# The first feed-forward product in block products of 256 columns, and sums of weight quadrants by adding DMAs

## The chip, the core and the metric

The kernel runs on one core of a Trainium2 chip. A core has five engines that run side by side, each with its own queue of instructions: TensorE (matmuls, PE in the profile, its weight loads PEld), VectorE (DVE), ScalarE (ACT), GpSimd (POOL) and SyncE (SP, which here only issues DMAs). The metric is the device time of one execution in microseconds; lower is better.

## The reference

One layer of a hybrid decoder: 512 tokens (S) of 1,024 channels (D), all in 32-bit floats.

```python
def hybrid_layer(x, norm1_w, w_in, ..., w_out, norm2_w, w_ff1, w_ff2, rel_bias):
    h = rmsnorm(x, norm1_w)
    proj = h @ w_in
    ...
    mix = jnp.concatenate([y_a.reshape(Bsz, S, A_WIDTH), y_b, y_c.reshape(Bsz, S, C_WIDTH)], axis=-1)
    x = x + mix @ w_out
    h2 = rmsnorm(x, norm2_w)
    x = x + jnp.square(jax.nn.relu(h2 @ w_ff1)) @ w_ff2
    return x
```

`y_a`, `y_b`, `y_c` are dilated attention, gated linear attention and block-sparse attention. A last RMSNorm follows. `w_ff1` is 1,024 x 4,096 and `w_ff2` 4,096 x 1,024. The change concerns the last line, from `h2` on.

## The kernel before

**Precision.** Every large product is made of three matmuls. A factor is split into a high part (rounded to a shorter format, by ScalarE) and a low part (what is left, by VectorE), and high x high, high x low and low x high are summed in PSUM. Splitting a weight tile of 128x1024 ("a cut", `parts`, lines 302 to 318) is one `wh` by ScalarE and one `wl` by VectorE. At most five cut pairs are alive (`WPAIRS`).

**The planner.** The order of every engine's queue is settled when the kernel is built. `Plan` (lines 105 to 202) runs some dozens of generators ("streams") that yield operations, waits for named events, and takes of counted resources (PSUM banks, cut pairs, large tiles). At each step it issues the operation that could start first by its cost formulas (lines 46 to 87), by priority among equals. So an edit of one stream can move instructions of others. All instructions are issued from one line (L137 in the profile), and rows are told apart by tile names. `order` rows below are this written order.

**Buffers.** 27 tiles of 128x1024 (`BIGS`, name tag "big") and 34 of 128x512 (`SLOTS`) are handed round.

**The stages.** Attention and its projections come first, until 191.9 us. Then `ff2(0)`, lines 1356 to 1401, multiplies the mixed heads by `w_out`. `y_out` (lines 1075 to 1094) transposes the normed tokens to `yh`, `yl`. `ffn` (lines 1313 to 1354) follows: the first product in 32 blocks `f` of 128 output columns, each of 8 k-tiles x 3 matmuls with all 512 tokens as the moving side (`f<-yh,wh 128x512`). Only blocks 0 to 3 go in two halves of 256 tokens, so as to start on the tokens that are ready first: 192 matmuls of 256 columns. The other 28 blocks are 672 matmuls of 512. `h_out` puts relu and square of a block into `h` tiles.

**The second product.** `w_ff2` is taken in four pieces c = 1 to 4 of 1,024 rows; `w_out` is c = 0. `ff2(c)` is a Strassen-Winograd product: two by two blocks, seven block products (24 matmuls of 512 columns each) where eight would be plain. The left factors are sums of the quadrants of `h` (`a_parts`, lines 1103 to 1178: `s` tiles, cut into `Ah`, `Al`), the right factors are sums of quadrants of the weights. Those sums, eight of 128x1024 per piece, are VectorE operations in `sums2` (lines 399 to 427): `w2raw<-w2raw`, `t<-w2raw`, `w2raw<-t,w2raw`, `w2raw<-w2raw,t`. The seven products accumulate in PSUM banks called `f2X`, `f2Y`, `f2Z`, `f2W`; VectorE adds a bank to the result rows `x` where Winograd's sums ask for it (`add`, lines 1183 to 1199), while later products go on in the same bank. `ff2(c)` for c = 1 to 3 comes after block f = 8c, `ff2(4)` after block 31.

**Loads.** SyncE's queue loads weights in 512 KB tiles: `wraw` for the first product (`fetch`, line 285), eight `w2raw` per piece (`fetch2`, lines 341 to 351). GpSimd's queue issues only a few small loads early on.

Of the kernel before, what the change touches and what calls it, by code (L numbers as in the profile page):

```python
# [28 lines left out]
BIGS, SLOTS, WPAIRS, SCRATCH = 27, 34, 5, 4096  # L29
NC = 5  # L30
# [3 lines left out]
def part_name(ap):  # L34
    name = ap.tensor.name
    if name[:2] in ("xh", "xl"):
        return f"{name}:{ap.offset // 512 % 4}"
    if name[:2] in ("yh", "yl"):
        return f"{name}:{ap.offset // 256 % 2}"
    return name  # L40


class Op:


    def __init__(self, eng, method, args, kw):
# [159 lines left out]
def hybrid_block_kernel(ctx: ExitStack, tc: tile.TileContext, x0_d, xT_d, x_d, w0_d, wv_d, wqk_d, w1_d, w2_d,  # L206
# [9 lines left out]
    plan = Plan(nc, dict(BANKS, raw=3, w=WPAIRS, big=BIGS, raw2=8, part=5, lev=4, cnt=1, few=1))  # L216
# [31 lines left out]
    cst = consts.tile([128, 1028], F32)  # L248
    ident = cst[:, 0:128]
    hsel = cst[:, 128:132]  # L250
    bmask = cst[:, 132:388]
    smask = cst[:, 388:900]
    flip = cst[:, 900:1028]
    lmask = consts.tile([128, len(LEVELS), 64], I32)
# [5 lines left out]
    gw = consts.tile([128, 256], F32)  # L260
# [9 lines left out]
    plan.free["big"].pop()  # L270
# [3 lines left out]
    xh, xl = ([t[:, k] for t in (quarters(n, F32R), quarters(n, F32R)) for k in range(4)] for n in ("xh", "xl"))  # L274
# [49 lines left out]
    def cut():  # L324
        for key, src, n in pieces:
            if key[0] in ("x", "x3"):
                continue
            yield ("wait", ("raw", key))
            yield from parts(key, raws.pop(key), n)
            give("raw")  # L330
            give("big")
            if key[0] == "1" and (key[1] % 8 == 0 and key[1] or key[1] == 31):
                yield from cut2((key[1] + 7) // 8)
            if key == ("v", 1, 3):
                yield from cut2(0)

# [4 lines left out]
    def fetch2():  # L341
        yield ("wait", ("raw", ("1", 5)))
        for c in range(1, NC):
            for q in ((0, 0), (1, 0), (1, 1), (0, 1)):
                for ip in range(2):
                    yield ("take", "raw2")
                    yield ("take", "big")
                    t = quads[c, q, ip] = big("w2raw")
                    yield SP.dma_start(t, w2_d[c, q[0], q[1], ip])
                fire(("quad", c, q))  # L350
            spawn(sums2(c), 4)
# [47 lines left out]
    def sums2(c):  # L399

        for q in ((0, 0), (1, 0), (1, 1), (0, 1)):
            yield ("wait", ("quad", c, q))
        b11, b12, b21, b22 = ([quads.pop((c, q, ip)) for ip in range(2)] for q in ((0, 0), (0, 1), (1, 0), (1, 1)))
        t2 = [None, None]
        B[c] = {0: b11, 1: b21, 5: b22, 3: b12, 2: t2, 4: b11, 6: b21}
        for n in (0, 1, 5):
            fire(("B", c, n))
        if c == NC - 1:
            yield ("prio", 2)
# [5 lines left out]
        fire(("B", c, 2))  # L415
        fire(("B", c, 3))
        yield ("wait", ("cut2", c, 0))
        for ip in range(2):
            yield DVE.tensor_tensor(b11[ip], t2[ip], b11[ip], op=OP.subtract)
        fire(("B", c, 4))  # L420
        yield ("wait", ("cut2", c, 1))
        for ip in range(2):
            yield DVE.tensor_tensor(b21[ip], b21[ip], t2[ip], op=OP.subtract)
        fire(("B", c, 6))
        yield ("wait", ("cut2", c, 2))
        give("big")
        give("big")

    B = {}

    def products(c):


        if not c:
            return ((0, "X", True, ((0, 0),)), (4, "W", True, ((1, 1),)), (6, "W", False, ((1, 0),)), (2, "X", False, ((1, 0),)),
                    (3, "X", False, ((1, 1),)), (1, "Y", True, ((0, 0),)), (5, "X", False, ((0, 1),)))
        if c < NC - 1:
            return ((0, "X", True, ((0, 0),)), (1, "Y", True, ((0, 0),)), (2, "X", False, ((0, 1),)), (3, "Z", True, ((1, 1),)),
                    (4, "X", False, ((1, 1),)), (5, "Z", False, ((0, 1),)), (6, "X", False, ((1, 0),)))
        return ((0, "X", True, ((0, 0),)), (4, "W", True, ((1, 1),)), (1, "Y", True, ((0, 0),)), (6, "W", False, ((1, 0),)),  # L440
                (2, "X", False, ((1, 0),)), (3, "X", False, ((1, 1),)), (5, "X", False, ((0, 1),)))

    def cut2(c):
        for o, (n, *_) in enumerate(products(c)):
# [58 lines left out]
    def load_small():  # L503
        yield ("wait", "zeros")
        for t, d in ((cst, cst_d), (rbx[:32], rb_d[:32]), (rb[64:67, :12], rb_d[32:]), (bav, ba_d), (wax[:16], wa2_d)):
# [65 lines left out]
    vB = [slot(f"vB{i}", shape=(128, 2, 256)) for i in range(2)]  # L571
    vS = {}
# [996 lines left out]
```

## Time and profile before

| what | value |
|---|---|
| median of 3 runs | 579.65 us (579.02, 579.65, 580.02) |
| the profiled execution's own time | 580.01 us |
| its span, first to last instruction | 577.9 us |
| mean granted TensorE clock | 0.999 |
| first product, blocks 4 to 31 | 672 matmuls of 512 columns |
| second product, each piece | 168 matmuls of 512 columns |

The span leaves out 2.1 us around it. The busy share of an engine is a mean over stages; what a stage is worth is read from the chain of waits (the work that ended last, followed back) and from windows of the stage. In a row of a group, "busy us, mean ns | idle before <- releaser" follows the shape; the mean of one operation includes a part that overlaps with the next one, so the distance between starts of operations that stand back to back is a little shorter. Granted clock and DMA share run from 0 to 1.

### The profile page before, as it was taken

To read this page: it belongs to the slowest core of one execution; us is meant where nothing else is said; L and a number is where in the kernel's file an instruction comes from. 1 tells how busy PE (TensorE), PEld (TensorE's weight loads), DVE (VectorE), ACT (ScalarE), POOL (GpSimd) and SP (SyncE) were. 2 spreads that over 40 slices of the span, in tenths; PEclk is the share of its full clock that TensorE was granted. 3 is DMA by queue.
4 is the path that set the end of the run, shared out by engine and by line. 5 is a ranking of instruction groups with operands and counts; after the bars stand their busy time and mean duration, and the time that the engine had idled before them with its cause. 6 is when DMAs were issued, how large, how long until landed. Compare 5 with 4: busy or idle time off the path is not lost.

```text
span 577.9 us, 8055 instructions
## 1 busy us (share of the span) xinstructions
PE 569.4 (99%) x3006; PEld 474.8 (82%) x3006; DVE 444.5 (77%) x774; ACT 329.3 (57%) x575; POOL 18.7 (3%) x36
## 2 busy tenths in 40 slices
PE   9999999999999999999999999999999999999995
PEld 8987888878888678899888888888888888888884
DVE  6879999897887889965399854599834698772995
ACT  6755566887777476636285435375253664273654
POOL 7100000000000000000000000000000000000021
PEclk9999999999999999999999999999999999999999
DMA  8921213430621435822007721028520057001004
GB/s 306 389 77 38 74 44 122 128 96 15 251 79 37 131 124 155 319 75 73 1 7 240 224 76 36 2 76 265 158 85 0 1 182 219 36 1 36 1 0 146
DMA packets 20838, 62.51 MB, mean 108 GB/s; under 512 B 2498, under 2 KB 3184, under 8 KB 20800
## 3 DMA queue, kind: packets, MB, share of 16 engines
q1 hardware_dynamic: 19872, 60.37, 31.9%
q0 software_dynamic: 640, 1.10, 0.6%
q8 instruction: 24, 0.39, 0.3%
q10 hardware_dynamic: 288, 0.53, 0.2%
q14 instruction: 14, 0.11, 0.1%
HBM read 59.86 MB, written 2.13 MB: 107 GB/s over the span
## 4 chain that ended last, share of the span: by engine, by line
PE 96%; DMA 2%; DVE 1%; issue 0%; ACT 0%; DVEq 0%
PE f L137 30%; PE f2X L137 17%; PE qkps L137 11%; PE vps L137 8%; PE f2Z L137 6%; PE f2Y L137 4%; PE f2W L137 4%; PE sps L137 3%; PE ptp L137 2%; PE po L137 2%; PE av L137 2%; DMA w2raw<-in_w 2%; PE lp L137 1%; PE bk L137 1%; PE bq L137 1%; PE op L137 1%
## 5 line engine op out<-in xcount | busy, mean ns | idle before, releaser
L137 PE MATMUL f<-yh,wh 128*128 128x512 f32 (+1 forms) x288 | 105.7, 367 | 0.0
L137 PE MATMUL f<-yl,wh 128*128 128x512 f32 (+1 forms) x288 | 105.5, 366 | 0.2 <-DVE yl L137 0.2
L137 PE MATMUL f<-yh,wl 128*128 128x512 f32 (+1 forms) x288 | 105.4, 366 | 0.0
L137 DVE TENSOR_TENSOR wl<-w2raw,wh 128x1024 fp32r<-128x1024 f32 x48 | 59.4, 1244 | 52.4 <-ACT wh L137 30.3
L137 DVE TENSOR_TENSOR wl<-wraw,wh 128x1024 fp32r<-128x1024 f32 (+1 forms) x60 | 68.4, 1152 | 24.5 <-ACT wh L137 24.3
L137 ACT ACTIVATE wh<-wraw 128x1024 fp32r<-128x1024 f32 (+1 forms) x59 | 58.0, 1002 | 30.4 <-PE f2X L137 18.6
L137 ACT ACTIVATE wh<-w2raw 128x1024 fp32r<-128x1024 f32 x48 | 50.4, 1054 | 32.9 <-PE f L137 14.5
L137 PE MATMUL f2X<-wh,Ah 128*128 128x512 f32 (+1 forms) x160 | 62.3, 390 | 0.0
L137 PE MATMUL f2X<-wl,Ah 128*128 128x512 f32 (+1 forms) x160 | 61.9, 387 | 0.0
L137 PE MATMUL f2X<-wh,Al 128*128 128x512 f32 (+1 forms) x160 | 61.9, 387 | 0.0
L137 PEld LDWEIGHTS f<-yl,wh 128*128 128x128 f32 x288 | 54.4, 189 | 9.1 <-DVE yl L137 0.4
L137 PEld LDWEIGHTS f<-yh,wl 128*128 128x128 f32 x288 | 54.3, 189 | 8.8
L137 PEld LDWEIGHTS f<-yh,wh 128*128 128x128 f32 x288 | 54.4, 189 | 8.7
L137 ACT ACTIVATE h<-f 128x512 f32<-128x512 f32 x32 | 19.0, 594 | 68.9 <-PE f L137 68.8
L137 PE MATMUL qkps<-xh,wh 128*128 128x512 f32 x96 | 39.2, 408 | 0.0
L137 PE MATMUL qkps<-xh,wl 128*128 128x512 f32 x96 | 37.6, 392 | 0.0
L137 PE MATMUL qkps<-xl,wh 128*128 128x512 f32 x96 | 37.5, 391 | 0.0
L137 PEld LDWEIGHTS f2X<-wh,Ah 128*128 128x128 f32 x160 | 30.1, 188 | 7.6 <-issue 1.6
L137 PEld LDWEIGHTS f2X<-wl,Ah 128*128 128x128 f32 x160 | 30.1, 188 | 6.2
L137 PEld LDWEIGHTS f2X<-wh,Al 128*128 128x128 f32 x160 | 30.1, 188 | 6.0
L137 ACT ACTIVATE P<-P,mn 128x512 f32<-128x512 f32 (+3 forms) x48 | 26.5, 553 | 14.6 <-DVE mn L137 14.5
L137 DVE TENSOR_TENSOR x<-f2X,x 128x512 f32<-128x512 f32 (+1 forms) x41 | 26.8, 674 | 6.5 <-PE f2X L137 6.3
(247 smaller groups left out, 1148.7 us busy)
## 6 DMA issues: line engine op xcount, KB each, us to landing
wraw<-in_w SPq DMA_DIRECT2D x32, 512.0 KB, 4.2
w2raw<-in_w SPq DMA_DIRECT2D x32, 512.0 KB, 4.3
wraw<-in_wqk SPq DMA_DIRECT2D x12, 512.0 KB, 4.4
wraw<-in_wv SPq DMA_DIRECT2D x8, 512.0 KB, 8.8
woraw<-in_w SPq DMA_DIRECT2D x8, 512.0 KB, 7.6
nb<-tab SPq DMA_DIRECT2D x12, 256.0 KB, 3.8
x<-in_x SPq DMA_DIRECT2D x8, 256.0 KB, 4.1
wraw<-in_w SPq DMA_DIRECT2D x7, 264.0 KB, 5.6
```

What stands on the lines that cost most here:

```text
L137: getattr(getattr(self.nc, op.eng), op.method)(*op.args, **op.kw)
```

## The change

**First product.** It becomes eight units of 512 output columns. Unit 0 is computed as blocks 0 to 3 were. Units 1 to 7 are Strassen-Winograd products as well: k in two halves, the unit's columns in two halves of 256, the tokens in two halves of 256. Each of seven block products has 24 matmuls of 256 columns: `f1V`, `f1W`, `f1X` are the banks, in the order V, W, V, X, V, W, V. After products 0, 1 and 2 ScalarE copies the bank to a kept tile `up`; after products 3, 4 and 5 VectorE adds that to the bank (`h<-f1X,up` and so on) before relu and square; the last one goes straight to relu. A later product in the same bank waits for that copy or add.

```diff
+            for n, (b_, new, after) in enumerate((("V", True, None), ("W", True, None), ("V", False, 0), ("X", True, None),
+                                                  ("V", False, 2), ("W", False, 1), ("V", False, 4))):
+                yield ("wait", ("w", ("1", u, n)))
+                yield ("wait", ("U", n))
...
+                if after is not None:
+                    yield ("wait", ("uy", u, after))
...
+            if n < 3:
+                t = kept[n] = slot("up")
+                yield ACT.activation(t, bk["VWV"[n]], AF.Copy)
+                fire(("uy", u, n))
+            elif n == 3:
+                yield ("wait", ("uy", u, 0))
+                yield from total(0, 1, bk["X"], kept[0], "g")
+            elif n == 4:
+                yield from total(1, 0, bk["V"], kept[1], None)
```

**Its factors.** The right factors are quadrants of the first matrix and four sums of them per unit, VectorE operations of 128x1024 (`sums1`); a unit has seven cuts, where 512 columns had four. The left factors are quadrants of the transposed tokens and four sums of them, made once: `y_out` now also copies each transposed piece uncut (`yr`, by ScalarE) before it gives the bank back, and `y_sums` makes four sums `yt`, `yr` and cuts them to `Uh`, `Ul`.

```diff
         yield ACT.activation(hi, src, AF.Copy)
         yield DVE.tensor_tensor(lo, src, f32(hi), op=OP.subtract)
-        give(r)
         for k in range(half * 4, half * 4 + 4):
             fire(("y", t, k))
+        yield ACT.activation(raw, src, AF.Copy)
+        give(r)
...
+        s1 = B1[u][1] = big("w1sum")
+        yield DVE.tensor_tensor(s1, a21, a22, op=OP.add)
+        fire(("B1", u, 1))
+        yield ("wait", ("cut1", u, 0))
+        yield DVE.tensor_tensor(a21, a11, a21, op=OP.subtract)
```

**Sums of the second matrix.** The VectorE sums of pieces 1 to 4 are gone. A quadrant is loaded by SyncE, and another is added to it by a DMA with an add, issued from GpSimd's queue, 512 KB each. The tile B22 + B12 is cut for product 4; when that cut is done, B11 is added to it and it is cut for product 2; then (c < 4) B21 is added and it is cut for product 6. B12 + B11 is another tile, for product 3. That is 8 adding DMAs for c = 1, 2, 3 and 12 for c = 4 (product 6 has a tile of its own there), 36 in all, and 10, 10, 10 and 12 plain loads where there were 8 each. Signs in `a_parts` and `add` change with the sums.

```diff
-        for ip in range(2):
-            yield DVE.tensor_tensor(b12[ip], b12[ip], b11[ip], op=OP.subtract)
-            yield ("take", "big")
-            t2[ip] = big("t2")
-            yield DVE.tensor_tensor(t2[ip], b22[ip], b12[ip], op=OP.subtract)
...
+        def added(ts, q):
+            for ip in range(2):
+                yield POOL.dma_start(ts[ip], w2_d[c, q[0], q[1], ip], accum_op=OP.add)
...
+            for i, (n, q) in enumerate(zip(ns, ((0, 1), (0, 0), (1, 0)))):
+                if i:
+                    yield ("wait", ("cut2", c, ns[i - 1]))
+                yield from added(ts, q)
+                fire(("B", c, n))
```

**Second products.** `ff2(c)` follows directly on unit 2c - 1. For c = 1 to 3 the order of the block products becomes 0, 4, 1, 2, 3, 5, 6 (banks X, W, Y, X, X, X, W) where it was 0 to 6 (X, Y, X, Z, X, Z, X). Products 2, 3 and 5 finish the first half of the rows' tiles before the second for all c, as c = 4 had it.

```diff
-            return ((0, "X", True, ((0, 0),)), (1, "Y", True, ((0, 0),)), (2, "X", False, ((0, 1),)), (3, "Z", True, ((1, 1),)),
-                    (4, "X", False, ((1, 1),)), (5, "Z", False, ((0, 1),)), (6, "X", False, ((1, 0),)))
...
+        m = ((0, "X", True, ((0, 0, 1),)), (4, "W", True, ((1, 1, -1),)), (1, "Y", True, ((0, 0, 1),)), (6, "W", False, ((1, 0, 1),)),
+             (2, "X", False, ((1, 0, 1),)), (3, "X", False, ((1, 1, -1),)), (5, "X", False, ((0, 1, -1),)))
+        return m if c == NC - 1 else m[:3] + m[4:] + m[3:4]
```

**Buffers.** Many small tiles of the attention part move into halves of large ones:

```diff
-BIGS, SLOTS, WPAIRS, SCRATCH = 27, 34, 5, 4096
+BIGS, SLOTS, WPAIRS, SCRATCH = 43, 22, 5, 2048
```

**What it does to the written order.** In the rows, `x_2400`, `x_2412`, `x_2417`, `x_2419`, `x_2460`, `x_2476`, `x_2478`, `x_2480` (before: `x_2425` and so on) are the eight result tiles, `s_` tiles sums of quadrants of `h`.

VectorE where the first product starts, before: the last `yl` (the transposed tokens' low parts), then sums of the second matrix and the first cuts.

```order
446 L137 SCALAR_TENSOR_TENSOR y_2937<-x_2489,y,nw_2472 128x512
447 L137 TENSOR_TENSOR yl<-yps,yh 128x4x128 x2
448 L137 TENSOR_TENSOR w2raw<-w2raw 128x1024
449 L137 TENSOR_TENSOR t_3012<-w2raw 128x1024
450 L137 TENSOR_TENSOR w2raw<-w2raw 128x1024
451 L137 TENSOR_TENSOR t_3036<-w2raw 128x1024
452 L137 TENSOR_TENSOR wl<-wraw,wh 128x1024 x4
453 L137 TENSOR_TENSOR Al<-h,Ah 128x512 x2
454 L137 TENSOR_TENSOR s_3195<-h 128x512
455 L137 TENSOR_TENSOR s_3200<-h 128x512
```

And now:

```order
425 L139 TENSOR_TENSOR yl<-yps,yh 128x4x128 x2
426 L139 TENSOR_TENSOR yt<-yr 128x1024
427 L139 TENSOR_TENSOR w1raw<-w1raw 128x1024
428 L139 TENSOR_TENSOR w1raw<-w1sum,w1raw 128x1024
429 L139 TENSOR_TENSOR Ul<-yt,Uh 128x1024
430 L139 TENSOR_TENSOR yt<-yr 128x1024
431 L139 TENSOR_TENSOR yr<-yr,yt 128x1024
432 L139 TENSOR_TENSOR Ul<-yr,Uh 128x1024
433 L139 TENSOR_TENSOR yr<-yr 128x1024
434 L139 TENSOR_TENSOR wl<-w1sum,wh 128x1024
435 L139 TENSOR_TENSOR Ul<-yt,Uh 128x1024
436 L139 TENSOR_TENSOR Ul<-yr,Uh 128x1024
437 L139 TENSOR_TENSOR wl<-w1raw,wh 128x1024 x2
```

The sums of the second matrix are gone from here; behind the last `yl` stand the sums and cuts of the token quadrants (`yt`, `yr`, `Ul`) and of the first unit's weights.

VectorE at the end of the first stretch, before: the cuts of the second matrix for `ff2(1)`, with its sums among them.

```order
456 L137 TENSOR_TENSOR wl<-w2raw,wh 128x1024 x2
457 L137 TENSOR_TENSOR w2raw<-t_3012,w2raw 128x1024
458 L137 TENSOR_TENSOR w2raw<-t_3036,w2raw 128x1024
459 L137 TENSOR_TENSOR wl<-w2raw,wh 128x1024 x2
460 L137 TENSOR_TENSOR w2raw<-w2raw,t_3012 128x1024
461 L137 TENSOR_TENSOR Al<-h,Ah 128x512 x2
462 L137 TENSOR_TENSOR s_3339<-h 128x512
463 L137 TENSOR_TENSOR s_3344<-h 128x512
464 L137 TENSOR_TENSOR s_3353<-s_3339,h 128x512
```

And now the end of unit 1 (`h<-f1V,up`) and the first cuts of `ff2(1)`:

```order
450 L139 TENSOR_TENSOR h<-f1V,up 128x512
451 L139 TENSOR_TENSOR wl<-w2raw,wh 128x1024
452 L139 TENSOR_TENSOR h<-f1W,up 128x512
453 L139 TENSOR_TENSOR wl<-w2raw,wh 128x1024
454 L139 TENSOR_TENSOR Al<-h,Ah 128x512
455 L139 TENSOR_TENSOR wl<-w2raw,wh 128x1024
456 L139 TENSOR_TENSOR Al<-h,Ah 128x512
457 L139 TENSOR_TENSOR s_3469<-h 128x512 x2
458 L139 TENSOR_TENSOR x_2400<-f2X,x_2400 128x512
459 L139 TENSOR_TENSOR x_2412<-f2X,x_2412 128x512
460 L139 TENSOR_TENSOR s_3483<-s_3469,h 128x512 x2
461 L139 TENSOR_TENSOR wl<-w2raw,wh 128x1024 x2
```

The two cuts at 451 and 453 are those for product 4, and the second cut at 461 is that for product 2, from the same tile after its add. No sum of the second matrix is left; the adds of the units' partial results are new.

VectorE in the second half of `ff2(1)`, before, where banks X and Z took turns:

```order
488 L137 TENSOR_TENSOR Al<-s_3441,Ah 128x512
489 L137 TENSOR_TENSOR wl<-w2raw,wh 128x1024
490 L137 TENSOR_TENSOR x_2491<-f2Z,x_2491 128x512
491 L137 TENSOR_TENSOR x_2493<-f2Z,x_2493 128x512
492 L137 TENSOR_TENSOR Al<-h,Ah 128x512
493 L137 TENSOR_TENSOR wl<-w2raw,wh 128x1024
494 L137 TENSOR_TENSOR Al<-h,Ah 128x512
495 L137 TENSOR_TENSOR wl<-w2raw,wh 128x1024
496 L137 TENSOR_TENSOR x_2491<-f2X,x_2491 128x512
497 L137 TENSOR_TENSOR x_2493<-f2X,x_2493 128x512
```

And now, from the read of X behind product 2 on:

```order
474 L139 TENSOR_TENSOR x_2417<-f2X,x_2417 128x512
475 L139 TENSOR_TENSOR Al<-s_3575,Ah 128x512
476 L139 TENSOR_TENSOR wl<-w2raw,wh 128x1024
477 L139 TENSOR_TENSOR Al<-s_3575,Ah 128x512
478 L139 TENSOR_TENSOR x_2419<-f2X,x_2419 128x512
479 L139 TENSOR_TENSOR Al<-h,Ah 128x512
480 L139 TENSOR_TENSOR wl<-w2raw,wh 128x1024
481 L139 TENSOR_TENSOR x_2478<-x_2478,f2X 128x512
482 L139 TENSOR_TENSOR wl<-w2raw,wh 128x1024
483 L139 TENSOR_TENSOR Al<-h,Ah 128x512
484 L139 TENSOR_TENSOR x_2480<-x_2480,f2X 128x512
485 L139 TENSOR_TENSOR wl<-w2raw,wh 128x1024
```

Reads of X for products 2, 3 and 5 follow one another, with cuts for products 5 and 6 between them. On GpSimd's queue, 36 rows `DMA w2raw<-in_w 128x1024` are new. On TensorE the blocks' rows were of this form:

```order
1560 L137 MATMUL f_3669<-yl,wh 128x512
1561 L137 MATMUL f_3669<-yh,wl 128x512
1562 L137 MATMUL f_3669<-yh,wh 128x512
```

and the units' rows are:

```order
1410 L139 MATMUL f1V<-Uh,wh 128x256
1411 L139 MATMUL f1V<-Ul,wh 128x256
1412 L139 MATMUL f1V<-Uh,wl 128x256
1413 L139 MATMUL f2X<-wh,Ah 128x512
```

The last row is the first matmul of `ff2(1)`, which now follows directly on unit 1's last product.

More of the change, by code (lines that the diff above doesn't have):

```diff
@@ L269, in hybrid_block_kernel @@
     x0n = big("x0n")
-    plan.free["big"].pop()
+    masks = big("masks", shape=(128, 768))
+    bmask = masks[:, 0:256]
+    smask = masks[:, 256:768]
+    for _ in range(2):
+        plan.free["big"].pop()
     xT = [None] + [slot("xT") for _ in range(KT - 1)]
@@ L339, in hybrid_block_kernel, with cut1 @@
+    def cut1(u):
+        for n in range(7):
+            yield ("wait", ("B1", u, n))
+            yield from parts(("1", u, n), B1[u][n])
+            fire(("cut1", u, n))
+            for _ in range((0, 0, 1, 0, 1, 2, 1)[n]):
+                give("big")
+            for _ in range((0, 0, 0, 0, 1, 2, 1)[n]):
+                give("raw1")
     quads = {}
     def fetch2():
-        yield ("wait", ("raw", ("1", 5)))
+        yield ("wait", ("quad1", 1, (0, 1)))
         for c in range(1, NC):
-            for q in ((0, 0), (1, 0), (1, 1), (0, 1)):
+            last = c == NC - 1
+            B[c] = {}
+            for ns, q in (((0,), (0, 0)), ((4, 2) if last else (4, 2, 6), (1, 1)), ((1,), (1, 0)), ((6,), (1, 1)), ((3,), (0, 1)), ((5,), (1, 1))):
+                if ns == (6,) and not last:
+                    continue
+                ts = []
@@ L569, in bias_table @@
         fire("tab")
-    vB = [slot(f"vB{i}", shape=(128, 2, 256)) for i in range(2)]
-    vS = {}
+    vB = big("vB", shape=(128, 2, 2, 256))
+    vB = [vB[:, i] for i in range(2)]
+    plan.free["big"].pop()
+    vS, vT = {}, {}
     st = {}
@@ L661, in gla @@
         fire("b")
-        attn = [slot(f"attn{h}", shape=(128, NB, 128)) for h in range(4)]
+        attn = []
+        for _ in range(2):
+            yield ("take", "big")
+            a = big("attn", shape=(128, 2, NB, 128))
+            attn += [a[:, 0], a[:, 1]]
         lev = {}
@@ L736, in gla @@
         yield ops
+        for _ in range(3):
+            give("big")
         for i, r in enumerate("go"):
@@ L882, in values @@
             yield ops
+            for _ in range(4 + (ps_[0] == 0) + 2 * (ps_[0] == 4)):
+                give("big")
             for p, po, r in zip(ps_, pos, "og"):
@@ L950, in v_proj @@
                     give_w()
+                if t == NT - 1 and g and k % 2:
+                    give("big")
+                    give("big")
+                    if k > 4:
+                        give("w")
             if t == 0:
@@ L1098, in h_out, with square @@
+    hq = {}
+    def square(h, key):
+        yield Any(ACT.activation(h, h, AF.Square), DVE.tensor_tensor(h, h, h, op=OP.mult), late=dict(vector=1.0))
+        fire(("hq", *key))
+    def h_out(f, acc, r):
+        h = yield from halves(1, f)
         yield ACT.activation(h, split2(acc), AF.Relu)
         give(r)
+        key = 1, 0, f // 2
+        hq[key] = hq.get(key, 0) + 1
+        last = hq[key] == 2
         yield Any(ACT.activation(h, h, AF.Square), DVE.tensor_tensor(h, h, h, op=OP.mult), late=dict(vector=1.0))
-        fire(("h", c, f))
+        if last:
+            for half in range(2):
+                fire(("hq", *key, half))
@@ L1148, in a_parts @@
         yield from urgent(1)
-        if ends:
-            yield from split(4, s3)
+        yield from split(4, s3)
+        give("big")
         yield from urgent(2)
-        for f in range(4, 8):
-            yield ("wait", ("h", c, f))
+        yield from ready(1, 0)
         q10, q11 = quad(1, 0), quad(1, 1)
@@ L1165, in a_parts @@
         yield from urgent(5)
-        yield from split(3, s1)
+        yield from split(3, s1, -1 if c else 1)
+        give("big")
         yield from urgent(6)
@@ L1169, in a_parts @@
             yield from split(1, q10)
-        s4 = yield from made("s4", q10, s2, OP.subtract)
-        if not ends:
-            yield from split(4, s3)
+            s4 = yield from made("s4", q10, s2, OP.subtract)
+        else:
+            yield ("take", "big")
+            s4 = big("s4", F32, (128, 2, 2, 256))
+            s4 = [s4[:, ip] for ip in range(2)]
+            for ip in range(2):
+                yield DVE.scalar_tensor_tensor(s4[ip], q10[ip], -1.0, s2[ip], op0=OP.mult, op1=OP.subtract)
+        give("big")
         yield from split(5, s4)
-        if not ends:
+        give("big")
+        if c not in (0, NC - 1):
             yield from split(6, q11)
@@ L1189, in add @@
             for acc, cs in zip(accs, cols):
-                yield DVE.tensor_tensor(x3[t, half][:, cs], acc[:, :cs.stop - cs.start], x3[t, half][:, cs], op=OP.add)
-            if c in (0, NC - 1) and not any((blk, half) in p[3] for p in products(c)[i + 1:]):
+                a, x = acc[:, :cs.stop - cs.start], x3[t, half][:, cs]
+                yield DVE.tensor_tensor(x, a, x, op=OP.add) if sign > 0 else DVE.tensor_tensor(x, x, a, op=OP.subtract)
+            if c in (0, NC - 1) and not any((blk, half) == g[:2] for p in products(c)[i + 1:] for g in p[3]):
                 if not c:
@@ L1356, in ff2 @@
+        for u in range(8):
+            if u % 2 == 0:
+                spawn(a_parts(u // 2 + 1), 2)
+            yield from unit(u) if u else ff1_first()
+            if u == 7:
+                for _ in range(6):
+                    give("part")
+            if u % 2:
+                yield from ff2(u // 2 + 1)
     def ff2(c):
```

324 lines of the change are left out of this document (217 added, 107 removed).

## The prediction

> **What bounds the kernel now.** I read the page's totals first, then the chain of waits, then the windows and groups of the stages that the change rewrites.
>
> ```profile
> span 577.9 us, 8055 instructions
> PE 569.4 (99%) x3006; PEld 474.8 (82%) x3006; DVE 444.5 (77%) x774; ACT 329.3 (57%) x575; POOL 18.7 (3%) x36
> ...
> PE 96%; DMA 2%; DVE 1%; issue 0%; ACT 0%; DVEq 0%
> ```
>
> TensorE is busy for 99% of the span and is 96% of the chain that ended last. So removed matmul time is gained one for one, and any new wait of a matmul is lost one for one. What other engines do counts only where a matmul comes to wait for it. The chain in order of time gives the price of the matmuls concerned (start, us, what):
>
> ```profile
> 331.79 43.52 PE f L137 x192
> 375.31 5.44 PE f2X L137 x24
> ...
> 407.95 5.44 PE f2X L137 x24
> 413.39 43.52 PE f L137 x192
> ...
> 554.83 13.61 PE f2X L137 x60
> 568.47 0.04 DVE x L137
> ```
>
> A product of 512 columns goes at 43.52/192 = 0.2267 us. One period (eight column blocks, then one second product of seven block products) lasts 413.39 - 331.79 = 81.60 us: 43.52 and 7 x 5.44 = 38.08. Behind the chain's last matmul, at 568.47, lie 9.4 us of output work, which the change leaves alone. The same view at the first four column blocks, which run in halves of 256 columns:
>
> ```profile
> 249.92 12.12 PE f L137 x101
> ```
>
> That is 12.12/101 = 0.1200 us for 256 columns, more than half of 0.2267 (0.1133). The windows say why (us, then busy time and count of PE, PEld, DVE, ACT, POOL, then granted clock, DMA share, GB/s), first with 256, then with 512 columns:
>
> ```profile
> 250.00:266.00 16.00, 16.00 (x136) 16.00 (x135) 7.92 (x8) 6.53 (x9) 0.00 (x0) 1.00 0.20 68
> 266.00:293.00 27.00, 27.00 (x123) 22.43 (x122) 13.37 (x15) 12.05 (x18) 0.00 (x0) 1.00 0.08 24
> ```
>
> With 256 columns the weight load is busy all of the time, 16.00 of 16.00 us; with 512 it has gaps, 22.43 of 27.00. So 0.1200 us is what a pair of load and 256 columns costs here, at a full clock.
>
> **The matmuls.** The change takes away the 672 matmuls of 512 columns (blocks 4 to 31) and puts 7 units x 7 block products x 24 = 1,176 matmuls of 256 columns in their place; the orders shown above have them in that form. 672 x 0.2267 = 152.3 us go, 1,176 x 0.1200 = 141.1 come: **-11.2 us**. By period: the stretch before the first second product goes from 5 blocks, 27.2 us, to one unit, 168 x 0.1200 = 20.2; the next two from 43.5 to 40.3 each; the last from 38.1 to 40.3. The break-even pitch is 152.3/1,176 = 0.1295 us.
>
> The Trainium skill, "TensorE: Matmul & The Clock Gate", section "Back-to-back issue gap", gives for a lone warm matmul N/2.4 + 2.5 ns: 215.8 ns for 512 and 109.2 for 256. By it, as an estimate, the exchange would be 128.4 - 145.0 = -16.6 us. The trace disagrees at 256 columns, 0.1200 us with the loader full, so I keep -11.2.
>
> **VectorE and ScalarE between.** The period that stays cyclic (two units and a second product), and the costs of one operation (groups: busy us, mean ns | idle before; then VectorE's timeline: start, busy):
>
> ```profile
> 332.00:414.00 82.00, 82.00 (x364) 67.93 (x363) 57.11 (x68) 39.66 (x53) 0.00 (x0) 1.00 0.34 104
> ...
> L137 ACT ACTIVATE wh<-w2raw 128x1024 fp32r<-128x1024 f32 x48 | 50.4, 1054 | 32.9 <-PE f L137 14.5 <-PE f2X L137 6.8 <-PE f2Y L137 4.6
> L137 ACT ACTIVATE h<-f 128x512 f32<-128x512 f32 x32 | 19.0, 594 | 68.9 <-PE f L137 68.8
> ```
> ```profile
> 376.66 1.22 DVE L137 TENSOR_TENSOR wl<-t,wh 128x1024 fp32r<-128x1024 f32 x1
> 377.80 0.69 DVE L137 TENSOR_TENSOR Al<-s,Ah 128x512 fp32r<-128x512 f32 x1
> 378.40 1.22 DVE L137 TENSOR_TENSOR w2raw<-w2raw,t 128x1024 f32<-128x1024 f32 x1
> ```
>
> Starts lie 377.80 - 376.66 = 1.14 us apart behind a 128x1024 operation, 0.60 behind a 128x512 one; these pitches I use. VectorE per period: minus the 8 sums of the second matrix, -9.1; 14 weight cuts for 8, +6.8; 8 sums of the first matrix, +9.1; 6 adds of kept partial results, +3.6. So 57.1 becomes 67.5 us in a period of 78.4: 86% where it was 70%. ScalarE gets 6 cuts (1.05) and 6 copies out of PSUM (0.59): 39.7 + 9.8 = 49.5 us, 63%. Neither is the bound by its sum, but VectorE's slack falls from 25 to 11 us, so four places need a look.
>
> *Start of unit 1.* All left factors of the units are made from the transposed activations. In the new order of VectorE 20 operations of 128x1024 and 8 of 128x512 stand from the last `yl` to the add `h<-f1V,up`, without which product 6 may not write its bank: 20 x 1.14 + 8 x 0.60 = 27.6 us. TensorE meanwhile has the second halves of unit 0, 96 x 0.1200 = 11.5, and products 0 to 5, 6 x 2.88 = 17.3: 28.8 us. With 1.2 us to spare and a hand-over from ScalarE ahead of many of them, I bound it by 0 and 3 and take 1.0.
>
> *Raw copies.* ScalarE copies each of eight transposed pieces once more before the bank is given back; the first copies cost
>
> ```profile
> L137 ACT ACTIVATE yh<-yps 128x512 fp32r<-128x512 f32 x8 | 4.6, 593 | 3.7 <-PE yps L137 3.7
> ```
> ```profile
> 242.94 0.38 PE L137 MATMUL f<-yl,wh 128*128 128x256 f32 x1 [0.22 <-DVE yl L137]
> ```
>
> 8 x 0.59 = 4.7 us more on an engine that TensorE waited for by way of `yl` for only 0.22 us there. The second halves of unit 0 (tokens 0 to 255) sit behind the last of them; 0 to 2, I take 0.3.
>
> *Windows inside a unit.* Products 2, 4, 5 and 6 wait for the copy or add of product 0, 2, 1 and 4. The product or products between give 2.88 us (8.64 for 5), against a copy of 0.59 behind one cut of 1.05, or an add of 0.60 behind one of 1.14: 1.7 us. I take 0. With two cuts ahead it is 2.9, and the cover is gone; 0.3 us at half of the 28 windows, 4 us, is the other end.
>
> *Second half of a second product.* Products 2, 3 and 5 now follow one another on the same X banks. From the first read of X behind product 2 to the last behind product 5, VectorE's new order has 9 operations of 128x512 and 7 of 128x1024, 13.4 us, beside 2.5 products of TensorE, 13.6. A bank's read has half a product, 2.7 us, before the next writes it. Bounds 0 and 2 for each of the three; I take 0.7 in all.
>
> **Adding DMAs.** Where VectorE formed the sums, GpSimd's queue now issues 36 DMAs that add 512 KB to a loaded tile. The trace has none. Its nearest rows are the plain loads on SP's queue and the largest one on GpSimd's (KB each, us to landing):
>
> ```profile
> w2raw<-in_w SPq DMA_DIRECT2D x32, 512.0 KB, 4.3
> cst<-in_cst POOLq DMA_DIRECT2D x1, 514.0 KB, 7.2
> ...
> GB/s 306 389 77 38 74 44 122 128 96 15 251 79 37 131 124 155 319 75 73 1 7 240 224 76 36 2 76 265 158 85 0 1 182 219 36 1 36 1 0 146
> ```
>
> From 4.3 us (an add for free) to 2 x 7.2 = 14.4 (twice GpSimd's load); I take 8.6, two plain loads, nearest to the row of the same tile. The second tile of a pair comes a little later: at 319 GB/s 512 KB take 1.6 us, so 3.3 for double traffic, 12 us for the pair. What it may take: the tile of product 4 is cut, then B11 is added, then it is cut for product 2. VectorE's first cut stands ahead of the add `h<-f1W,up`, so TensorE has product 6 of the unit, 2.88, and products 0, 4 and 1, 16.3, before product 2: 19.2 us, less the two halves of a cut, 1.05 + 1.14, and some hand-over: **about 16.5**. For product 6 it is much the same (products 2, 3 and 5, 16.3, and the lead that the cuts have). VectorE's own cover is smaller: 3 x 1.14 + 9 x 0.60 = 8.8 us to its next cut of that tile. Behind that waiting cut stand an `Al<-s` for product 2 and the read of W, so a longer add eats VectorE's lead at first and TensorE's time only from 16.5 us. I take 1.0 us in all, with 0 and 7 as ends (one us on each of the seven chained pairs). GpSimd's issues cost little:
>
> ```profile
> 6.08 0.74 POOL L137 DMA_DIRECT2D cst<-in_cst  x1
> 43.34 0.52 POOL L137 DMA_DIRECT2D tab<-vals  x1 [27.25 <-DVE vals L137]
> ```
> ```profile
> 42.97 0.40 DVE L137 TENSOR_TENSOR kq<-kB,e 128x256 f32<-128x256 f32 x1
> 43.30 0.41 DVE L137 TENSOR_TENSOR kq<-qB,e 128x256 f32<-128x256 f32 x1
> 43.64 0.74 DVE L137 TENSOR_TENSOR e<-b 128x256 f32<-128x256 f32 x2
> ```
>
> 36 x 0.74 = 27 us on an engine that is busy for 18.7. The loads: 16 tiles of 512 KB in a period before, now 8 + 10 plain and 8 adding ones, 26 to 34 tiles' worth. The DMA share of 0.34 becomes 0.34 x 26/16 x 82/78.4 = 0.58 to 0.76: not full, cover for a landing that is some us later.
>
> **Buffers.** The attention part's tiles move from slots to big tiles (34 slots to 22, 27 big tiles to 43). Its matmuls and their order stay; I take 0, within 2 either way.
>
> **The sum.** -11.2 + 1.0 + 0.3 + 0.7 + 1.0 = -8.2. The profiled execution took 580.01 us (its span of 577.9 and 2.1 around it); 0.4 above the median of 579.65. So 571.8 for such an execution and **571.4** against the median. A difference of 0.2%, 1.2 us, is the least that counts here as a change.
>
> **Rivals.**
>
> *The adding DMAs are slow (slower).* If a pair takes P us, TensorE waits P - 16.5 at each chained pair: products 2 and 6 in three second products, product 2 in the last, seven in all. Against -11.2 and 2.0 for the rest the gain is gone at P = 16.5 + 9.2/7 = 17.8; with 19 it is -11.2 + 2.0 + 17.5 = +8.3, or **588**. For it: no row shows an add, and GpSimd's load at 7.2 us was slower than SP's at 4.3. Against: 12 us is the estimate, and GpSimd's issue at 43.34 took 0.52 us amid VectorE's two-input operations. The Trainium skill, "SBUF — State Buffer", sections on the "DVE blocks DMA" trap and "Who interferes with whom", has GpSimd's descriptors wait while VectorE runs a copy, cast or tensor_scalar in a two-port mode, and holds that tensor_tensor has none; the row at 43.34 agrees, and nearly all of VectorE's work here is tensor_tensor. Chance 0.09.
>
> *VectorE falls behind in the second products (less gain).* The groups show how its cuts wait:
>
> ```profile
> L137 DVE TENSOR_TENSOR wl<-w2raw,wh 128x1024 fp32r<-128x1024 f32 x48 | 59.4, 1244 | 52.4 <-ACT wh L137 30.3 <-PE f L137 22.1
> ```
>
> 30.3/48 = 0.6 us for ScalarE per cut. If only 0.3 of it stays at the seven large operations beside products 2, 3 and 5, 2.1 - 0.2 of slack = 1.9 us three times: 5.7 more, **577**. Against: TensorE never waited in such a stretch before, with VectorE 94% busy from 375 to 414 (36.72 of 39.00 us):
>
> ```profile
> 375.00:414.00 39.00, 39.00 (x174) 32.32 (x173) 36.72 (x46) 22.63 (x28) 0.00 (x0) 1.00 0.57 175
> ```
>
> Chance 0.14.
>
> *The pitch grows.* If the loader, already full, slips to 0.127 to 0.1295 us with weights that DMAs and two engines write more often, the matmuls bring 2.9 to 0 us and the 3.0 of waits remain: **580 to 582.5**. The row 250 to 266 had a DMA share of only 0.20. Chance 0.04.
>
> *The pitch is half of that of 512 columns.* 1,176 x 0.1133 = 133.3: -19.0 + 3.0, **564**. It is what the skill's formula tends to; the full loader row speaks against it. Chance 0.02.
>
> **How the numbers follow.** The forecast has 0.71, 568.0 (no wait at all: 579.65 - 11.2 = 568.45, and a little for buffers) to about 575 (waits of 6 to 7 us, half of the sum of their upper ends without the DMAs': 3 + 4 + 2 + 6 = 15). The range goes on to 578.5 to take in most of the second rival; the slow adds, both pitches and its tail, 0.18, stay out. Faster: 0.71 + 0.02 + 0.13 of the second rival = 0.86. Same: 0.01 of that, 0.02 of the grown pitch, 0.02 of adds just past 17 us = 0.05. Slower: 0.07 + 0.02 = 0.09.
>
> **What the changed profile would show.** Right: 1,176 matmuls `f1V`, `f1W`, `f1X` at 0.120 us with PEld full; units of 20.2 us in the chain; VectorE 84 to 88% busy in a period; idle time of PE outside the first 30 and last 10 us below 4 us; adding DMAs landing in 6 to 12 us. Wrong: PE waiting at product 2 or 6 of a second product for `wh` behind a DMA (slow adds); at products 3 and 5 for `x<-f2X` (VectorE behind); at product 6 of unit 1 for the add; or a unit above 21 us without a wait (pitch).

## The result and the profile after

The changed kernel takes 569.08 us (median of 4 runs, 568.69 to 569.85) against 579.57 for the kernel before: a ratio of 0.9821, 95% interval 0.9804 to 0.9838. The profiled execution took 569.85 us with a span of 568.1. That is 10.5 us less by the medians, where -8.2 were forecast: inside the range, and past the forecast by most of the 3.0 us of waits that were added to it.

The head of the page (busy time and share of each engine, then the chain):

```profile
span 568.1 us, 9233 instructions
...
PE 558.8 (98%) x3510; PEld 489.7 (86%) x3510; DVE 485.7 (86%) x819; ACT 367.9 (65%) x630; POOL 51.9 (9%) x73
...
PE 95%; DVE 2%; issue 1%; ACT 1%; DVEq 0%
```

TensorE is still the chain. The chain in order of time, from the first second product of the feed-forward on (start, us, what):

```profile
288.01 5.47 PE f2X L139 x24
...
304.36 16.32 PE f2X L139 x72
320.68 5.44 PE f2W L139 x24
326.12 2.87 PE f1V L139 x24
329.00 2.88 PE f1W L139 x24
...
366.44 5.47 PE f2X L139 x24
...
444.85 5.47 PE f2X L139 x24
...
545.06 13.61 PE f2X L139 x60
```

Each piece begins where the one before it ends. A period is 444.85 - 366.44 = 78.41 us (78.40 forecast), a product of 24 matmuls 2.88 us, or 0.1200 each, and from 250.59 us to the chain's last matmul, which ends at 558.67, there is no gap. So the exchange of matmuls brought 11.2 us as worked out. The window of that period, and what TensorE waited for in the whole execution (us in total, times, longest):

```profile
366.40:444.80 78.40, 78.40 (x506) 71.83 (x505) 67.42 (x79) 48.02 (x65) 7.14 (x9) 1.00 0.66 175
```
```profile
PE warm L139 <- DVE eps L139: 1.1, 1, 1.1
PE yps L139 <- DVE y L139: 1.1, 2, 0.6
PE vps L139 <- ACT rg L139: 0.6, 1, 0.6
```

VectorE has 67.42 us of 78.40 (67.5 forecast), ScalarE 48.02 (49.5), the DMA share is 0.66 (0.58 to 0.76). The first and third waits were there before. Only `yps` is new, 1.1 us at two transposes, before unit 1. The adding DMAs:

```profile
w2raw<-in_w SPq DMA_DIRECT2D x42, 512.0 KB, 5.8
w2raw<-in_w POOLq DMA_DIRECT2D x36, 512.0 KB, 6.8
```

They land after 6.8 us at the median, where 8.6 was taken between ends of 4.3 and 14.4. (A second trace of the same kernel has 7.3.)

The account of the spans: -11.2 for the matmuls. In the chain, the X products of `ff2(0)` begin at 217.55 us before and 217.81 after; the stretch behind unit 0 begins at 266.5 before (the first second product's 293.71 less 27.2) and at 267.86 after. So 1.1 us are lost between, and 0.3 ahead of it: -9.8, which is 577.9 to 568.1. The 0.3 may be chance: in the second trace of the changed kernel those X products begin at 218.16, 0.35 later still, while the stretch behind them takes the same 50.05 us (217.81 to 267.86, 218.16 to 268.21). The 10.5 us of the medians are 0.7 more than the spans; the profiled execution of the changed kernel was the slowest of its four, and the spans leave out some time around them.

### The profile page after: what moved, and what is told of

It reads as the page before. It is cut to its first block, busy times and chain, and to the rows that moved or that the text cites. A ratio compares the mean times of both kernels' runs of the same rounds, so it can differ in the third digit from the quotient of the medians.

```text
span 568.1 us, 9233 instructions
## 1 busy us (share of the span) xinstructions
PE 558.8 (98%) x3510; PEld 489.7 (86%) x3510; DVE 485.7 (86%) x819; ACT 367.9 (65%) x630; POOL 51.9 (9%) x73
## 4 chain that ended last, share of the span: by engine, by line
PE 95%; DVE 2%; issue 1%; ACT 1%; DVEq 0%
PE f2X L139 18%; PE f1V L139 14%; PE qkps L139 12%; PE f2W L139 10%; PE vps L139 8%; PE f1W L139 7%; PE f2Y L139 4%; PE f1X L139 4%; PE f L139 3%; PE sps L139 3%; PE ptp L139 2%; PE po L139 2%; PE av L139 2%; PE lp L139 1%; PE bq L139 1%
## 5 line engine op out<-in xcount | busy, mean ns | idle before, releaser
L139 POOL DMA_DIRECT2D w2raw<-in_w x36 | 31.8, 904 | 409.7 <-DVE wl L139 190.8
L139 DVE TENSOR_TENSOR wl<-w1raw,wh 128x1024 fp32r<-128x1024 f32 x42 | 50.8, 1221 | 12.7 <-ACT wh L139 12.7
L139 ACT ACTIVATE wh<-w1raw 128x1024 fp32r<-128x1024 f32 x42 | 43.3, 1051 | 28.2 <-DVE w1raw L139 26.5
L139 PE MATMUL f1V<-Uh,wh 128*128 128x256 f32 x168 | 47.5, 283 | 0.0
L139 PE MATMUL f1V<-Ul,wh 128*128 128x256 f32 x168 | 47.5, 283 | 0.0
L139 PE MATMUL f1V<-Uh,wl 128*128 128x256 f32 x168 | 47.5, 283 | 0.0
L139 ACT ACTIVATE h<-h 128x512 f32<-128x512 f32 x53 | 33.3, 629 | 18.9 <-DVE h L139 18.3
L139 PEld LDWEIGHTS f2X<-wh,Ah 128*128 128x128 f32 x160 | 30.1, 188 | 7.5 <-issue 1.6
L139 DVE TENSOR_TENSOR wl<-wraw,wh 128x1024 fp32r<-128x1024 f32 (+1 forms) x32 | 34.8, 1092 | 1.5 <-ACT wh L139 1.3
L139 PEld LDWEIGHTS f2X<-wh,Al 128*128 128x128 f32 x160 | 30.1, 188 | 5.7
L139 PEld LDWEIGHTS f1V<-Uh,wh 128*128 128x128 f32 x168 | 32.3, 192 | 0.0
L139 PEld LDWEIGHTS f1V<-Ul,wh 128*128 128x128 f32 x168 | 32.3, 192 | 0.0
```

Source lines behind the costliest of these rows:

```text
L139: getattr(getattr(self.nc, op.eng), op.method)(*op.args, **op.kw)
```

## The experiments

**Was VectorE's relief needed?** One part undone:

```diff
-        def added(ts, q):
-            for ip in range(2):
-                yield POOL.dma_start(ts[ip], w2_d[c, q[0], q[1], ip], accum_op=OP.add)
...
+        for ip in range(2):
+            yield DVE.tensor_tensor(b12[ip], b12[ip], b11[ip], op=OP.add)
+            yield ("take", "big")
+            t2[ip] = big("t2")
+            yield DVE.tensor_tensor(t2[ip], b22[ip], b12[ip], op=OP.add)
```

> One part undone: the changed kernel with the second matrix's sums back on VectorE (eight of 128x1024 per piece, eight plain loads, no adding DMA). In the changed profile VectorE is busy 67.4 of the 78.4 us of a period. Theory (the adding DMAs are what makes room for the block products): 8 x 1.14 = 9.1 us more make 76.5 of 78.4, 98%, with all its hand-overs; TensorE waits 2 to 4 us in each of the four second products, 577 to 585 us. Rival (VectorE had room for both, the adding DMAs were not needed): below 78.4 it still fits, TensorE never waits, 569 to 570 us.

Measured: 578.79 us (0.9989 of before, 0.998 to 0.9999). The time is the theory's and its rival falls: without the adding DMAs nearly the whole gain is gone. The window of a period, and the two longest of TensorE's new waits:

```profile
367.00:447.00 80.00, 78.77 (x507) 71.83 (x506) 75.91 (x87) 48.29 (x65) 0.00 (x0) 1.00 0.33 106
```
```profile
PE f2X L139 <- DVE wl L139: 3.8, 3, 1.3
PE f1V L139 <- ACT wh L139: 1.1, 1, 1.1
```

VectorE is busy for 75.91 of 80.00 us, and the chain runs through it in the first three second products up to product 2; two of them:

```profile
304.96 0.60 DVE s L139
305.56 1.15 DVE wl L139
306.75 14.82 PE f2X L139 x64
...
386.71 14.80 PE f2X L139 x64
```

A period is 386.71 - 306.75 = 79.96 us, 1.55 more than with the adding DMAs. The places are not quite the theory's: against the changed kernel the first three second products are longer by 1.5 to 1.6 us each and the last one by nothing; the two units ahead of the last one are longer by 2.6, and the work behind TensorE's last product by 2.0.

A share of 95% does not by itself make an engine the bound. Here are the first 20 us of a pair of units and of a second product, in the changed kernel and then with the sums on VectorE:

```profile
326.00:346.00 20.00, 20.00 (x169) 20.00 (x168) 13.05 (x14) 9.34 (x14) 0.00 (x0) 1.00 0.45 139
366.40:386.40 20.00, 20.00 (x90) 16.55 (x89) 19.34 (x27) 13.24 (x19) 2.54 (x3) 1.00 0.80 156
```
```profile
327.00:347.00 20.00, 20.00 (x169) 20.00 (x168) 18.33 (x20) 12.26 (x17) 0.00 (x0) 1.00 0.23 80
367.00:387.00 20.00, 18.77 (x84) 15.29 (x83) 19.31 (x26) 14.14 (x20) 0.00 (x0) 1.00 0.18 56
```

In the second product VectorE is as full in both, 19.34 and 19.31 us of 20.00, and TensorE waits in one of them only. The units differ, 13.05 and 18.33: there VectorE has room to get ahead in the changed kernel, and nearly none with the sums.

**Is the relief worth something by itself?** One part alone, in the kernel before (with `products`, `a_parts` and signs to go with it):

```diff
-            spawn(sums2(c), 4)
...
+                if ns[0] in (0, 1, 5):
+                    fire(("B", c, ns[0]))
+                else:
+                    spawn(sums2(c, ns), 4)
```

> One part alone: the kernel before, with its first product in 28 blocks of 512 columns, but with the second matrix's sums made by adding DMAs and with the new order and signs of the second product. Theory (TensorE did not wait for VectorE before, so relief of VectorE is worth nothing by itself): 579.6 us, within 0.5, VectorE down by 9.1 us a period. Rival (the sums or the old order of products cost TensorE something): 577 us or less. Third case (adding DMAs land too late where VectorE runs far ahead): 581 us or more.

Measured: 579.41 us (0.9999, 0.9989 to 1.0008): the theory. Its window:

```profile
332.00:414.00 82.00, 82.00 (x364) 67.89 (x363) 48.55 (x59) 38.60 (x53) 7.01 (x8) 1.00 0.62 169
```

VectorE falls from 57.11 to 48.55 us and the time does not move. So neither part is worth much alone: the block products without room on VectorE bring 0.7 us (579.50 for before on that chip), the room without them nothing, both together 10.5.

**How late may an add be?** First B11 is added twice, and three times (3 in place of 2 below), in a row:

```diff
-                yield from added(ts, q)
+                for _ in range(2 if i == 1 else 1):
+                    yield from added(ts, q)
```

> The suspected wait doubled: the changed kernel, but B11 is added twice, one add behind the other, to the tile of product 2 of each second product (so the result holds it twice). Adds land in 6.8 us each at the median, so the chain from the cut for product 4 to that for product 2 takes about 14 us and some more for the pair. Theory (TensorE's lead of 16.5 us is the cover): 569 to 570.5 us. Rival (VectorE's own 8.8 us is the cover, what comes later is lost): (14 - 8.8) us at four second products, about 590 us.

Measured: 580.17 us, 11.1 more than the changed kernel, between the theories. The chain at the first second product:

```profile
297.83 4.77 PE f2Y L139 x21
...
302.63 0.69 DVE x L139
...
304.53 0.59 DVE s L139
305.12 1.15 DVE wl L139
306.31 14.80 PE f2X L139 x64
```

No DMA is in it. The planner, which reckons with the second add, had written a cut for product 2 behind the reads of Y, and these wait for product 1. TensorE lost 1.5 to 1.6 us in each of the first three second products by an order, not by a landing. The rest came in the units before the last one, 1.9 us, and in the last one, 4.4, where no DMA is in the chain either; the first one began 1.1 us earlier. So the run does not tell the two covers apart.

> The same with three adds in a row: about 21 to 24 us for the chain. Theory (cover 16.5 us): TensorE waits 5 to 8 us at product 2 of each of four second products, 589 to 600 us, and the wait is named as one for the cut of product 2. Rival (the lead is longer, or the queue hides it): under 575 us.

Measured: 603.25 us, a little beyond the theory's range, 34.2 more than the changed kernel. In the trace the first three second products are longer by 9.5 to 10.5 us each and the last one by 3.5. The planner's order is another one here too, but now the wait is for the adds: TensorE's weight load (PEld) waits for ScalarE's cut, and the cut for the DMA:

```profile
ACT wh L139 <- DMA w2raw<-in_w: 28.1, 8, 5.0
...
PEld f2X L139 <- ACT wh L139: 19.7, 7, 3.7
```

To have the double add without a new order, its cost was taken out of the planner alone:

```diff
+            for o in more:
+                o.free = True
+            yield ops[0]
+            yield [ops[1]] + more
...
+        if getattr(op, "free", False):
+            return at
```

> Again B11 added twice to the tile of product 2 (the result holds it twice), but now every engine's written order is that of the changed kernel; only GpSimd's queue has eight adding DMAs more. In the run with two adds before this one the cut of product 2 was also written later, behind the reads of Y, and TensorE waited 2.8 us there. Theory (what decides is TensorE's lead, 16.5 us, against 6.0 + 6.8 and the pair's second tile): the cut for product 2 comes 2 to 5 us later, TensorE waits 0 to 1 us at it, 569 to 572 us. Rival (the add itself is late, whatever the order): 2.8 us four times again, 580 us.

Measured: 575.88 us, 6.8 more than the changed kernel: again neither. The four second products are longer by 2.3, 2.0, 1.3 and 1.2 us in the trace. VectorE's and ScalarE's orders are those of the changed kernel. GpSimd's queue shows the two adds of the first tile (the first and third row; the second row is the second tile's), and VectorE's queue the cut that waits for them:

```profile
284.76 0.88 POOL L139 DMA_DIRECT2D w2raw<-in_w  x1 [41.39 <-DVE wl L139]
287.17 0.88 POOL L139 DMA_DIRECT2D w2raw<-in_w  x1 [1.53 <-DVE wl L139]
291.03 0.87 POOL L139 DMA_DIRECT2D w2raw<-in_w  x1 [2.98 <-DMA w2raw<-in_w]
```
```profile
299.03 1.23 DVE L139 TENSOR_TENSOR wl<-w2raw,wh 128x1024 fp32r<-128x1024 f32 x1 [2.60 <-ACT wh L139]
```

In the chain the second add lands at 297.85, 13.1 us after the first was issued. The cut begins at 299.03. In the changed kernel the first add was issued, and the cut made, at

```profile
284.88 0.89 POOL L139 DMA_DIRECT2D w2raw<-in_w  x1 [40.27 <-DVE wl L139]
```
```profile
295.33 2.36 DVE L139 TENSOR_TENSOR wl<-w2raw,wh 128x1024 fp32r<-128x1024 f32 x2
```

The cut is the second of that pair, which stands without a wait: it begins 1.14 us behind the row's start, at 296.47. So the doubled add makes it 2.6 us late. Product 2 began at 304.36 in the changed kernel, long after either, yet TensorE now has:

```profile
PE f2X L139 <- DVE x L139: 5.3, 4, 1.9
```

VectorE stood idle ahead of that cut, everything written behind it moved, and the read of X behind product 2 came too late for product 3. So the cover of an add is the time from its issue to VectorE's next cut of that tile, 296.47 - 284.88 = 11.6 us less the 1.07 of ScalarE's half: about 10.5 us here. Lateness beyond it is passed on to TensorE for the most part: 2.3 us of 2.6 in this second product, 2.0 of 2.4 in the next, 1.3 of 2.0 in the third. The lead of 16.5 us covers the cut, not what stands behind it.

**What does the add itself cost?** The same DMAs without it:

```diff
-                yield POOL.dma_start(ts[ip], w2_d[c, q[0], q[1], ip], accum_op=OP.add)
+                yield POOL.dma_start(ts[ip], w2_d[c, q[0], q[1], ip])
```

> The add alone taken away: the same 36 DMAs of 512 KB on GpSimd's queue, to the same tiles at the same places, as plain loads (so the tiles hold the last quadrant instead of the sum). Theory (a double read makes an add about 1.5 to 2 us longer than a plain load, and all of it is covered): landing 4.5 to 5.5 us where the adds had 6.8, time as the changed kernel, 569.1 us within 0.6. Rival (the adds hold up other loads and with them TensorE somewhere): 567.5 us or less.

Measured: 568.83 us, the theory.

```profile
w2raw<-in_w POOLq DMA_DIRECT2D x36, 512.0 KB, 4.6
```
```profile
L139 POOL DMA_DIRECT2D w2raw<-in_w x36 | 19.1, 530 | 418.7 <-DVE wl L139 197.9
```

The changed kernel's row is

```profile
L139 POOL DMA_DIRECT2D w2raw<-in_w x36 | 31.8, 904 | 409.7 <-DVE wl L139 190.8
```

Landing takes 4.6 instead of 6.8 us, an issue 530 instead of 904 ns. The add costs 2.2 us of latency, and none of it is paid: from unit 1's first matmul to the end both kernels take 300.2 us (266.80 to 567.0 here, 267.86 to 568.1 there), and TensorE has no wait in it. GpSimd's order is the same in both; that of VectorE and ScalarE is not, as the planner reckons a plain load as shorter.

**Where did 1.1 us go before unit 1?** ScalarE's queue there, in the changed kernel:

```profile
236.06 0.60 ACT L139 ACTIVATE yr<-yps 128x512 f32<-128x512 f32 x1 [0.76 <-DVE yl L139]
236.56 0.62 ACT L139 ACTIVATE junk<-x 128x512 f32<-128x512 f32 x1
...
238.75 0.60 ACT L139 ACTIVATE yr<-yps 128x512 f32<-128x512 f32 x1 [0.99 <-DVE yl L139]
```

The raw copies wait for VectorE's `yl`, and behind the first stands `junk`, the sum of squares that the next tokens' norm, and with it the next transpose, needs. Two runs take the copies away and move them:

```diff
-        yield ACT.activation(raw, src, AF.Copy)
         give(r)
...
```

> The changed kernel without the eight raw copies of the transposed tokens: their sums are formed from the rounded high parts instead (so the sums lack the low parts). Theory (the copies on ScalarE stand ahead of the sums of squares, and with them TensorE's 1.1 us of waits at the transposes): first second product of the feed-forward begins 1 us earlier, 568.0 us. Rival (that time went with the buffers or the loads in front): 569.1 us.

Measured: 567.41 us, 1.7 below the changed kernel: the theory, by more than expected. From the X products of `ff2(0)` to unit 1 it takes 48.5 us (216.89 to 265.37), 1.6 less than the changed kernel.

```diff
-        yield ACT.activation(raw, src, AF.Copy)
-        give(r)
-        fire(("yr", t, half))
+        def later():
+            yield ACT.activation(raw, src, AF.Copy)
+            give(r)
+            fire(("yr", t, half))
+
+        spawn(later(), 2)
```

> The same work as the changed kernel, but each raw copy is a stream of its own with a lower priority, so that the planner may put other work of ScalarE ahead of it. Theory (the copies' place costs about 1 us): 568.2 to 568.8 us. Rival (a later copy holds its bank longer and delays unit 1's sums): 569.1 us or more.

Measured: 568.07 us. As the two medians came from different chips, the pair was run together once more:

> The changed kernel once more, as the partner of the next run on one chip: 569.1 us within 0.6.

> The raw copies as streams of lower priority once more, beside the changed kernel on the same chip. Theory (the place of the copies costs about 1 us): 0.8 to 2 us below its partner. Rival (the two medians of different chips misled): within 0.5 us of it.

Measured: 569.73 us (569.01 to 570.30) for the changed kernel and 567.86 (567.56 to 568.36) with the copies later, 1.9 below it. Against before this is 0.9799 (0.9786 to 0.9812). It is the fastest of the kernels that leave nothing out. The window of the transposes, first of the changed kernel, then with the copies later:

```profile
228.00:252.00 24.00, 22.95 (x146) 20.00 (x145) 22.58 (x43) 16.84 (x38) 3.58 (x4) 1.00 0.91 252
```
```profile
228.00:252.00 24.00, 24.00 (x158) 21.41 (x158) 23.95 (x45) 17.96 (x40) 3.58 (x4) 1.00 0.87 244
```

TensorE's missing 1.05 us is back, at the same work. The stretch from the X products of `ff2(0)` to the first matmul of unit 1 takes 48.6 us (217.57 to 266.15), 1.5 less than in the changed kernel. The other 0.4 of the 1.9 us lie ahead of it, where two traces of the changed kernel differ by 0.35 as well.

**What sets 0.120 us?** The prediction read it as the weight load's time. The units' matmuls with fewer columns:

```diff
-                        yield [PE.matmul(bk[b_][:, i * 256:i * 256 + 256], ww[:, w_], xx[:, k], start=(new and i + k + m == 0),
+                        yield [PE.matmul(bk[b_][:, i * 256:i * 256 + (256 if new and k + m == 0 else 192)], ww[:, w_], xx[:, k, :256 if new and k + m == 0 else 192], start=(new and i + k + m == 0),
```

> The pitch by itself: the matmuls of units 1 to 7 read 192 columns instead of 256 (all but the first of a bank; the last 64 columns lack most of their sum). Theory (the weight load, busy all of the time, sets 0.120 us): inside a unit a product still takes 2.88 us, total 568 to 569 us. Rival (the columns set it, 256 at one rate): 0.120 x 192/256 = 0.090 us, 2.2 us a product, and the period falls to VectorE's 67 us.

Measured: 560.76 us. The chain inside a unit, and the window:

```profile
328.91 2.68 PE f1V L139 x24
331.59 2.69 PE f1X L139 x24
```
```profile
324.00:349.00 25.00, 25.00 (x225) 25.00 (x225) 17.11 (x19) 15.58 (x23) 0.00 (x0) 1.00 0.42 131
```

2.68/24 = 0.1117 us: both theories fall. With 128 columns:

> As the run with 192 columns, now with 128 columns (all but the first matmul of a bank; the last 128 columns lack most of their sum). There a matmul took 2.68/24 = 0.1117 us, neither the 0.120 of a loader bound at 256 nor the 0.090 of columns alone. Theory (256 and 512 columns lie on one line, 0.0133 us and 0.417 ns a column, and the weight load is a floor of about 0.111 us beneath it): 0.111 to 0.112 us again, a product 2.66 to 2.69 us. Rival (a second, flatter line through 192 and 256, 0.13 ns a column): 0.103 us, 2.47 us a product.

Measured: 561.16 us, and

```profile
330.07 2.68 PE f1V L139 x24
332.75 2.69 PE f1X L139 x24
```

the same 0.1117. So there is a floor of 0.1117 us, the same at 192 and 128 columns; that it is the weight load's is the likely reading, its row being full, but no run changes the load by itself. At 256 the pitch of 0.1200 lies above the floor, so there the columns count: a straight line through it and the 0.2267 of 512 columns has 0.417 ns a column and 0.0133 us for each matmul. At 192 columns that line would give 0.093, below the floor; as it goes through two points, no run tests it.

## Why the prediction was right

*The matmuls*, -11.2 us: right to the tenth, from two rows of the trace. The reason given for 0.1200, a full loader, was wrong: the loader was shown busy for all of the time at 0.1117 as well. It did no harm, since the price itself was measured; but the rival of a growing pitch was argued from a bound that does not bind. Both rivals of the pitch fell: it is 0.1200 in all units.

*VectorE and ScalarE by their sums*: right, 67.42 and 48.02 us of 78.40. That VectorE has room was right, and the run with the sums on VectorE shows how little: 9 us more and nearly all of the gain is gone.

*Start of unit 1*, 1.0: measured 0, but not by the margin that was worked out. From the end of the last `yl` (253.32) VectorE took 30.1 us to the end of the add, where 27.6 were counted, and TensorE 31.8 to product 6 (285.13), where 28.8 were: both were counted too short, by luck nearly alike. *Windows inside a unit*, 0: right. *Second half of a second product*, 0.7: measured 0; from the first of those reads to the start of the last VectorE took 13.9 us (307.26 to 321.15 in the first second product), where 13.4 were worked out beside 13.6, and no matmul waited. *Adding DMAs*, 1.0: measured 0. Each was an insurance against a queue that has little to spare, and none fell due.

*Raw copies*, 0.3: the one term that was too small. Against the kernel before, the stretch is 1.1 us longer; against the runs without the copies or with later ones, 1.5 to 1.6. What the prediction left out is the place: it counted only the work, 4.7 us, and the wait behind the last copies; the trace shows ScalarE waiting ahead of a copy, with the sum of squares for the next transpose behind it.

*Buffers*, 0: the part ahead of the stretch is 0.3 us longer, no more than two traces of one kernel differ there.

So the time was nearer to the end without waits than the forecast because 2.7 us of the 3.0 taken for waits were not needed, while the copies cost more than their share.

*The first rival* (slow adds) was wrong in its price. Its deciding point, a pair of 17.8 us, came from TensorE's lead of 16.5; the run with the same order shows time lost at 13.1 us for one tile, from a cover of about 10.5. With 6.8 us it didn't come to that. The Trainium skill, "SBUF — State Buffer", section "Who interferes with whom", holds that tensor_tensor has no two-port mode. That agrees with the trace, where adds amid VectorE's tensor_tensor work landed in 6.8 us.

*The second rival* (VectorE behind) did not happen in the changed kernel. The run with 9 us more on VectorE shows it falling behind, at a cut for product 2; the wait that the rival named, of product 3 for a read of X, shows in the run with the doubled add in the same order.

## What to carry to other kernels

Before giving a nearly full engine more work, look for what can leave it: here two edits that are worth 0.7 and 0 us alone are worth 10.5 together, because one makes the room that the other uses. Look for that room where the engine gets ahead, not only in the stretch where it is fullest. Measure a wait's cover on the in-order queue that will stand still behind it, not on the engine that needs the datum last: what is written behind the waiting instruction is late as well. And a busy share of 100% on a unit that works ahead of another does not show that it sets the pace; change the size and see which row follows.

## What the runs showed of the hardware

A DMA that adds 512 KB to a tile landed in 6.8 us at the median and took 904 ns to issue, a plain one at the same place in its queue 4.6 us and 530 ns. The landing varies: 7.3 us in the second trace of the changed kernel, 8.7 with the adds in the kernel before. 36 of them beside the loads brought the DMA share to 0.66 in a period without a wait of TensorE.

Matmuls of 192 and of 128 columns, each with a weight load, both took 0.1117 us; 256 columns took 0.1200 and 512 took 0.2267. The row of the weight load was full at 0.1117 and at 0.1200 alike.

In the run with three adds in a row TensorE stood still for 2 to 3 us at a time, and the granted clock (the last column but two) fell after it:

```profile
304.00:305.00 1.00, 0.00 (x0) 0.00 (x0) 1.00 (x2) 0.00 (x0) 0.00 (x0) 1.00 0.81 229
305.00:306.00 1.00, 0.00 (x0) 0.00 (x0) 0.00 (x0) 0.96 (x1) 0.00 (x0) 1.00 1.08 193
307.00:308.00 1.00, 0.93 (x2) 0.50 (x2) 0.35 (x1) 0.00 (x0) 0.29 (x1) 0.50 1.07 221
308.00:309.00 1.00, 1.00 (x4) 0.66 (x2) 0.00 (x0) 0.00 (x0) 0.58 (x1) 0.50 0.99 279
```

It is 0.50 there, and 0.976 over the whole execution, where the changed kernel has 0.999. So a longer wait costs more than itself: TensorE's waits for cuts in the second products add up to 19.2 us, and the span is 32.6 longer; the lower clock, by an estimate from these means, is 0.023 of 600.7, about 14 us. The Trainium skill, "TensorE: Matmul & The Clock Gate", section "What's actually happening", has the clock halve after an idle window of about 3.4 us. The halving agrees; the stillness ahead of it was only about 2.5 us here (303.67 to 306.15, by the profile's modelled ends), and no run here measures the threshold.
